# Moving ScalarE's late squares and stores, the last weight splits, and the sharing of the last scalings in a hybrid encoder block

## The chip, the cores and the metric

The kernel runs on one core of a Trainium2 chip. Its time is the device time in microseconds (us) of one execution; the median of three runs of the kernel before is 2010.85 us (2010.63 to 2011.96). A NeuronCore has a matrix engine (TensorE, PE in the profile, with its weight loads as PEld), three engines for elementwise work (VectorE or DVE, ScalarE or ACT, GpSimd or POOL) and SyncE (SP), which here only issues transfers. Sixteen DMA engines move data between the device memory and the core's own memory; transfers are issued from SP, ACT or POOL.

## The reference, cut to what matters

The input x has 512 rows of 2048 numbers in float32.

```python
h = rmsnorm(x, g_mix)
qa, ka, va, qb, kb, vb = split(h @ w_in)
mixed = concat(rmsnorm(mixer_a(qa, ka, va), g_out_a), rmsnorm(mixer_b(qb, kb, vb), g_out_b))
x = x + mixed @ w_out
h2 = rmsnorm(x, g_ffn)
gate, up = split(h2 @ w_gate_up)
x = x + (silu(gate) * up) @ w_down
return rmsnorm(x, g_final)          # x / sqrt(mean(x*x) + eps) * g_final, row by row
```

## The kernel before, in words

**Precision and form.** Every float32 product is made of three matmuls: each operand is split into a rounded part "hi" and a remainder "lo", and `mm3` (L238 to L240) adds hi·hi, hi·lo and lo·hi. So weights must be split before use: ScalarE makes hi (L774), VectorE makes lo (L777). Most of the large products also use a seven-product form for 2x2 blocks (m1 to m7), for which VectorE first adds or subtracts weight tiles (L814).

**Units.** The work of TensorE is a list of units. A unit is one weight tile (128 x 512) with the matmuls that use it: 12 matmuls in the first chunk (units 0 to 15), 6 in the seven-product blocks that follow. The last loop of the kernel runs over the units in order, and writes each engine's instructions in that order: squares of x (`row_squares`), loads and splits for units some way ahead (`prepare`), the unit's matmuls, its `post` and the hooks set for this unit number. Each engine works its own list from the top, so an instruction that must wait holds all behind it on its engine. hi runs about five units ahead in these blocks (`COLS_AHEAD`), lo one unit behind hi.

**The beginning.** The first chunk computes the k and v columns of mixer A from all 16 column slices of x. Its four result banks are copied out by ScalarE (L468, `post_plain`) and stored to device memory as kvA (L455). Beside this, slices of x are transposed and split (L333 to L335, and L352 to L357 in `x_split` and `x_sums`), and ScalarE squares x with a running sum (L369): 16 instructions, one for each column group g and row tile t. The last four (g = 3) come at units 15, 16, 17 and 18. `make_r1` at unit 20 makes 1/rms of the rows: a reduction and a scaling on VectorE, a power on GpSimd (L220), one more scaling on VectorE (L389). Its first reader is the copy of the first finished form of the next block (L862, after unit 23).

**Places.** Weight tiles, the copies of the first chunk and the tiles of x share a pool of places of 128 x 512 (`homes`). At unit 15 three are free, so the fourth copy of the first chunk goes to the place of the first one, and waits until that one is stored. The next three loads of SP's list go to the places of the second, third and fourth copy. The four places of the last group of x come free with its last square.

**The end.** The last block of the down projection ends with forms m5, m4, m3. Rows are in four tiles t of 128, columns in four chunks c of 512. After m4 the rows 2 and 3 are complete: `put_row` adds the bank to x1 (VectorE, L1200) and squares the result (ScalarE, L1197). `row_scale` makes 1/rms (reduction and scaling on VectorE, power on GpSimd), `write_rows` scales the four chunks and stores each with SP (L1222). Three chunks of each row tile have been multiplied by g_final before (`gained`, L1204), and need only the row scale; the fourth takes both at once on VectorE (L1217). Form m3 runs with rows 0 first; its second half, for rows 1, is held until the end (`finish`), so that rows 2, 3 and 0 can be finished beside it. For the last row tile, the sum over three chunks is made ahead.

Of the kernel before, what the change touches and what calls it, by code (L numbers as in the profile page):

```python
# [15 lines left out]
OP = mybir.AluOpType  # L16
# [3 lines left out]
P = 128  # L20
# [3 lines left out]
NT = S // P  # L24
KD = D // P
NC = D // 512
# [41 lines left out]
def encoder_block(ctx, tc, x, g_mix, w_in, g_q_a, g_k_a, g_out_a, g_out_b, w_out, g_ffn,  # L68
                  w_gate_up, w_down, g_final, c_ident, c_mask, c_axial, c_partial, out):
    nc = tc.nc  # L70
# [13 lines left out]
    def slot(base, dtype=F32, shape=(P, 512)):  # L84
        return sp.tile(list(shape), dtype, tag="s", name=nm(base))
# [14 lines left out]
    def release(*tiles):  # L100
        banks.extend(tiles)
# [201 lines left out]
    def hook(n, f):  # L303
        hooks.setdefault(n, []).append(f)
# [58 lines left out]
    x_ss = small(4 * NT)  # L363

    def row_squares(n):
        g, t = (3, n - KD + 1) if n >= KD - 1 else divmod(n - 3, NT)
        if 0 <= g < 4 and 0 <= t < NT:
            row = x_groups[g][:, t]
            nc.scalar.activation(row, row, AF.Square, accum_out=x_ss[:, 4 * t + g:4 * t + g + 1])  # L369
            if g in (1, 3) and t == NT - 1:  # L370
                homes.extend(x_groups[g][:, i] for i in range(NT))
# [82 lines left out]
    def store(name, t, src, eng=None):  # L454
        (eng or nc.gpsimd).dma_start(spill[name][t], src)  # L455
        stored[name] += 1
# [4 lines left out]
    def post_plain(name, ps, rows=range(NT)):  # L461
        for t in rows:
            e = homes.popleft() if name == "kvA" else slot("ev" + name)
            if name[:3] == "qkB":
                nc.scalar.activation(e[:, :256], ps[t][:, :256], AF.Copy, scale=r1["rs"][:, t:t + 1])
                nc.scalar.activation(e[:, 256:], ps[t][:, 256:], AF.Copy, scale=r1["r"][:, t:t + 1])
            else:
                nc.scalar.activation(e, ps[t], AF.Copy, scale=1.0 if name == "kvA" else r1["r"][:, t:t + 1])  # L468
# [444 lines left out]
    x1 = {}  # L913
# [194 lines left out]
    for f in range(0, NFF, 4):  # L1108
        box = gate_up_block(f)
# [31 lines left out]
    gfin = {}  # L1141
    fin = {}
    def down_block(first, pairs, cb, last):
        box = ColBlock(w_down, 2 * first * P, (cb * 1024, cb * 1024 + 512), pairs, KEPT, f"draw{pairs}",
                       close=finish if last else None)

        def add(form, i, j):
            def go():
                for t in range(2):
                    row = 2 * i + t  # L1150
                    e = in_turn(evs, EVICT, [P, 512], F32, "ev")
                    nc.scalar.activation(e, box.bank_of(form)[t], AF.Copy, scale=r2["r"][:, row:row + 1])  # L1152
                    nc.gpsimd.dma_start(x1_dram[2 * cb + j, row], e, accum_op=OP.add)  # L1153
                if form in LAST_OF_BANK:
                    box.done(form)
            box.after(form, 0, go)

        def put(form, i, j):
            box.after(form, 0, lambda: [put_row(2 + j, 2 * i + t, box.bank_of(form)[t]) for t in range(2)])

        add("m1", 0, 0)
        add("m7", 1, 1)
        add("m6", 1, 0)
        if last:
            done_rows = [(c, t) for c in range(2) for t in (2, 3, 0, 1)]
            for n in range(2):
                box.after("m7", 2 + 3 * n, lambda n=n: [load_gfin(n), load_x1(n, (2, 3)), load_x1(n, (0, 1))])
            box.after("m7", 7, lambda: [load_gfin(c) for c in (3, 2)])
            for n, (c, t) in enumerate(done_rows):
                box.after("m6", n - 2, lambda c=c, t=t: squares(c, t))  # L1170
                box.after("m6", n, lambda c=c, t=t: gained(c, t))
            box.after("m6", 2, lambda: [load_x1(3, (2, 3)), load_x1(2, (0, 1)), load_x1(2, (2, 3)), load_x1(3, (0, 1))])
            put("m2", 0, 0)
            put("m5", 1, 1)
            put("m4", 1, 0)
            for t in range(2):
                box.after("m4", -6 + t, lambda t=t: gained(2, t))
                box.after("m4", -4 + t, lambda t=t: gained(3, 2 + t))
            box.after("m4", 1, lambda: [row_scale(t) for t in (2, 3)])
        else:  # L1180
            add("m2", 0, 0)
            add("m5", 1, 1)
            add("m4", 1, 0)
            add("m3", 0, 1)
        return box

    def load_gfin(c):
        gfin[c] = slot("gfin")
        nc.gpsimd.dma_start(gfin[c], row_bcast(g_final[c * 512:(c + 1) * 512], 512))
# [9 lines left out]
    def put_row(c, t, ps):  # L1199
        nc.vector.scalar_tensor_tensor(x1[c, t], ps, r2["r"][:, t:t + 1], x1[c, t], op0=OP.mult, op1=OP.add)  # L1200
        squares(c, t)
# [7 lines left out]
        nc.vector.tensor_reduce(tot, fin[t], axis=AX.X, op=OP.add)  # L1209
        fin["r", t] = rsqrt_mean(tot, 1, D)  # L1210

    def write_rows(t, by_vector):
        r = fin["r", t]
        for c in sorted(range(NC), key=lambda c: ("y", c, t) in fin):
            y = x1[c, t]
            if ("y", c, t) not in fin:
                nc.vector.scalar_tensor_tensor(y, y, r, gfin[c], op0=OP.mult, op1=OP.mult)  # L1217
            elif c == by_vector:
# [3 lines left out]
            nc.sync.dma_start(out[0, t * P:(t + 1) * P, c * 512:(c + 1) * 512], y)  # L1222

    def finish(box):
        ps = box.bank_of("m3")
        write_rows(2, None)
        write_rows(3, None)
        put_row(3, 0, ps[0])
        for u in box.held:
            mm3(ps[1], cols(form_of("m3", u.i), P), (u.pair[:, 0], u.pair[:, 1]), False, u.i == box.pairs - 1, True)  # L1230
        row_scale(0)
        write_rows(0, None)
        pre = small(2)
        nc.vector.tensor_reduce(pre[:, :1], sums_of(1)[:, :NC - 1], axis=AX.X, op=OP.add)
        nc.vector.tensor_scalar(pre[:, 1:], pre[:, :1], 1.0 / D, EPS, op0=OP.mult, op1=OP.add)
        put_row(3, 1, ps[1])
        m = small(1)
        nc.vector.tensor_scalar(m, fin[1][:, NC - 1:NC], 1.0 / D, pre[:, 1:], op0=OP.mult, op1=OP.add)
        fin["r", 1] = small(1)
        nc.gpsimd.tensor_tensor(fin["r", 1], m, mhalf[:, :1], op=OP.pow)  # L1240
        write_rows(1, 2)

    first = 0
    for n in DOWN_PAIRS:
        next_forms(box, first, n)
        for cb in range(2):
            box = down_block(first, n, cb, (first + n, cb) == (NFF // 2, 1))
# [5 lines left out]
    done = {"load": 0, "side": 0, "hi": 0, "lo": 0}  # L1253
# [53 lines left out]
    for n, u in enumerate(units):  # L1307
        if n < KD:
            if n + 5 < KD:
                load_x(n + 5)  # L1310
            if n + 1 < KD:
                x_prep(n + 1)
            if 4 < n < 10:
                next(gains, None)
        if n < KD + 3:
            row_squares(n)
        prepare(n)
        for v in units[n + 1:n + 3]:
            if v.early is not None:
                v.early()  # L1320
                v.early = None
        u.mm(u)
        if u.post is not None:
            u.post()
        for f in hooks.pop(n, ()):
            f()
        credit = credit + HEAD_RATE[n >= attend[1]] if attend[0] <= n < attend[2] else 1.0
        while side and credit >= getattr(side[0], "cost", 1.0):
            f = side.popleft()
            credit -= getattr(f, "cost", 1.0)  # L1330
            f()
        if not side:
            credit = 0.0
# [54 lines left out]
```

## Time and profile before

| | |
|---|---|
| median of three runs | 2010.85 us (2010.63 to 2011.96) |
| the profiled execution | 2011.22 us, of which the span is 2009.4 us and 1.8 us lie around it |
| granted TensorE clock | 0.997 |
| PE busy | 1984.8 us, 99% |
| VectorE, ScalarE, GpSimd busy | 1562.4, 1114.6 and 127.4 us |
| moved by DMA | 390.61 MB, mean 194 GB/s |

The profile shows one execution. Times in its rows are us from the span's start. A row of the timeline gives start, duration, engine, source line, operation, and output and input by the program's names; in brackets stands the idle time of the engine before it, and whose end released it. Rows of the same kind that follow each other are merged, with their count (x2); the duration is then that of the whole stretch. The letter q behind an engine means its instruction queue (waits and DMA issues). Matmuls are pipelined: the duration of one overlaps the next, so the distance of two starts is what counts.

### The profile page before, as it was taken

The page shows a single profiled execution, that of the slowest core. Times are in us where ns is not written, and L with a number is a line of the kernel's source. Part 1 is how long each engine was busy: PE and PEld are TensorE (multiplying, and loading weights), DVE is VectorE, ACT ScalarE, POOL GpSimd, SP SyncE. Part 2 cuts the span into 40 slices and gives each one's busy share as a digit, 9 for nine tenths or more (in the row PEclk, how much of TensorE's full clock was granted, in tenths as well). Part 3 has the DMA queues.
Part 4 walks back from the last instruction along what each step waited for, and adds up shares of the span by engine and source line. Part 5 has one row for each costly group of instructions (what it writes and reads, how often), then busy time and mean ns, then how long its engine had stood idle before and what let it go on. Part 6 is the DMA issues. An engine that isn't in the chain of part 4 may idle for free. (4 is left out here: it accounts for less than half of the span.)

```text
span 2009.4 us, 27417 instructions
## 1 busy us (share of the span) xinstructions
PE 1984.8 (99%) x9019; PEld 1632.0 (81%) x9019; DVE 1562.4 (78%) x2781; ACT 1114.6 (55%) x1988; POOL 127.4 (6%) x157
## 2 busy tenths in 40 slices
PE   9999999999999999999999999999999999999998
PEld 7788888887788888888888888888888888788886
DVE  6877876667764698878878878878779987877967
ACT  8655345456544565555555545455555666666656
POOL 0000100000010000000000000000000121111121
PEclk9999999999999999999999999999999999999999
DMA  8577433335344645737647657558467799768765
GB/s 274 179 276 249 159 116 99 106 129 169 96 140 132 209 153 188 279 119 258 241 135 273 208 178 275 168 189 287 141 221 262 195 248 272 187 169 266 200 152 175
DMA packets 231391, 390.61 MB, mean 194 GB/s; under 512 B 21408, under 2 KB 70352, under 8 KB 231120
## 3 DMA queue, kind: packets, MB, share of 16 engines
q1 hardware_dynamic: 204880, 326.13, 48.4%
q0 software_dynamic: 14960, 33.04, 8.1%
q10 hardware_dynamic: 11408, 29.70, 4.2%
q8 instruction: 70, 1.15, 0.2%
q14 instruction: 73, 0.60, 0.1%
HBM read 325.08 MB, written 63.70 MB: 193 GB/s over the span
## 5 line engine op out<-in xcount | busy, mean ns | idle before, releaser
L238 PE MATMUL b<-tw,arena 128*128 128x512 f32 x2136 | 838.4, 392 | 2.2 <-ACT ev L1152 2.2
L239 PE MATMUL b<-tw,arena 128*128 128x512 f32 x2136 | 833.6, 390 | 2.8 <-DVE tw L777 2.6
L240 PE MATMUL b<-tw,arena 128*128 128x512 f32 x2136 | 832.9, 390 | 0.0
L774 ACT ACTIVATE tw<-raw 128x512 fp32r<-128x512 f32 x924 | 558.6, 628 | 436.6 <-DVE raw L814 285.9
L777 DVE TENSOR_TENSOR tw<-raw,tw 128x512 fp32r<-128x512 f32 x924 | 617.8, 685 | 172.4 <-ACT tw L774 169.5
L239 PEld LDWEIGHTS b<-tw,arena 128*128 128x128 f32 x2136 | 401.7, 188 | 89.2 <-DVE tw L777 7.4
L238 PEld LDWEIGHTS b<-tw,arena 128*128 128x128 f32 x2136 | 401.5, 188 | 84.6 <-ACT ev L1152 2.9
L240 PEld LDWEIGHTS b<-tw,arena 128*128 128x128 f32 x2136 | 401.4, 188 | 84.5 <-DVE arena L330 0.5
L814 DVE TENSOR_TENSOR raw<-raw,raw 128x512 f32<-128x512 f32 x528 | 360.5, 683 | 2.0 <-DMA raw<-in_w_gate_up_dram 2.0
L238 PE MATMUL b<-w,arena 128*128 128x512 f32 x368 | 146.1, 397 | 0.0
L239 PE MATMUL b<-w,arena 128*128 128x512 f32 x368 | 143.6, 390 | 0.7 <-DVE w L295 0.7
L240 PE MATMUL b<-w,arena 128*128 128x512 f32 x368 | 143.8, 391 | 0.0
L1153 POOL DMA_DIRECT2D x1d<-ev x76 | 66.4, 975 | 1150.0 <-ACT ev L1152 1135.6
L239 PEld LDWEIGHTS b<-w,arena 128*128 128x128 f32 x368 | 69.2, 188 | 15.3 <-DVE w L295 1.6
L240 PEld LDWEIGHTS b<-w,arena 128*128 128x128 f32 x368 | 69.1, 188 | 14.9
L238 PEld LDWEIGHTS b<-w,arena 128*128 128x128 f32 x368 | 69.2, 188 | 13.5
L774 ACT ACTIVATE tw<-stage 128x512 fp32r<-128x512 f32 x93 | 55.6, 627 | 41.0 <-DVE stage L814 30.6
L777 DVE TENSOR_TENSOR tw<-stage,tw 128x512 fp32r<-128x512 f32 x93 | 61.5, 684 | 13.6 <-ACT tw L774 13.6
L295 DVE TENSOR_TENSOR w<-raw,w 128x512 fp32r<-128x512 f32 x96 | 64.7, 684 | 6.0 <-ACT w L290 3.5
L230 DVE TENSOR_TENSOR pTl<-b,pTh 128x512 fp32r<-128x512 f32 x64 | 43.8, 686 | 29.6 <-ACT pTh L229 26.9
L290 ACT ACTIVATE w<-raw 128x512 fp32r<-128x512 f32 x96 | 58.3, 623 | 15.5 <-PE b L239 6.9
L357 DVE TENSOR_TENSOR pair<-pair 128x256 f32<-128x256 f32 x120 | 45.5, 420 | 26.2 <-ACT pair L1009 25.1
(189 smaller groups left out, 1748.9 us busy)
## 6 DMA issues: line engine op xcount, KB each, us to landing
raw<-in_w_gate_up_dram SPq DMA_DIRECT2D x616, 256.0 KB, 5.3
raw<-in_w_down_dram SPq DMA_DIRECT2D x176, 256.0 KB, 7.1
stage<-in_w_in_dram SPq DMA_DIRECT2D x114, 256.0 KB, 4.8
forms<-pair SPq DMA_DIRECT2D x22, 896.0 KB, 5.3
x1d<-ev POOLq DMA_DIRECT2D x76, 256.0 KB, 6.7
fr<-forms ACTq DMA_DIRECT2D x35, 512.0 KB, 6.1
raw<-in_w_in_dram SPq DMA_DIRECT2D x64, 256.0 KB, 4.4
raw<-in_w_out_dram SPq DMA_DIRECT2D x32, 512.0 KB, 4.7
```

Of the source, the lines that this page charges most:

```text
L230: nc.vector.tensor_tensor(lo, src, f32(hi), op=OP.subtract)
L238: nc.tensor.matmul(dst, ah, bh, start=start, stop=False, skip_group_check=chained)
L239: nc.tensor.matmul(dst, ah, bl, start=False, stop=False, skip_group_check=chained)
L240: nc.tensor.matmul(dst, al, bh, start=False, stop=stop, skip_group_check=chained)
L290: nc.scalar.activation(self.w[0], src, AF.Copy)
L295: nc.vector.tensor_tensor(self.w[1], self.src, f32(self.w[0]), op=OP.subtract)
L357: nc.vector.tensor_tensor(out, x, y, op=op)
L774: nc.scalar.activation(self.pair[:, 0], self.src, AF.Copy)
L777: nc.vector.tensor_tensor(self.pair[:, 1], self.src, f32(self.pair[:, 0]), op=OP.subtract)
L814: nc.vector.tensor_tensor(t[dst], t[src[0]], t[src[1]], op=OP.add if form == "m6" else OP.subtract)
L1153: nc.gpsimd.dma_start(x1_dram[2 * cb + j, row], e, accum_op=OP.add)
```

## The change

1. `row_squares`: the last four squares of x come at units 17, 19, 21 and 23 instead of 15 to 18, and `make_r1` at unit 23 instead of 20.
2. `post_plain`: the four stores of the first chunk are issued by GpSimd instead of ScalarE.
3. `last_weights`: after the last unit of form m4, and ahead of everything else that is hooked there, the hi and lo splits of all weights that are left are written.
4. `write`, `finish`: the scalings and stores of the end are written chunk by chunk. For rows 2 and 3 the chunk that takes both factors comes first, then two on ScalarE, and the last on VectorE behind `put_row(3, 0)`. For rows 0, one of three single scalings goes to VectorE. For rows 1 the fourth chunk is multiplied by g_final (into the place of another gain tile) while ScalarE squares it; VectorE then scales three chunks, ScalarE one, which ScalarE also stores.

```diff
     def row_squares(n):
-        g, t = (3, n - KD + 1) if n >= KD - 1 else divmod(n - 3, NT)
+        g, t = divmod(n - 3, NT)
+        if g >= 3:
+            late = n - KD - 1
+            g, t = (3, late // 2) if late >= 0 and late % 2 == 0 else (-1, 0)
...
-    hook(20, make_r1)
+    hook(23, make_r1)
...
-            store(name, t, e, nc.scalar)
+            store(name, t, e, None if name == "kvA" else nc.scalar)
...
             put("m5", 1, 1)
+            box.after("m4", 0, last_weights)
             put("m4", 1, 0)
...
+    def last_weights():
+        while done["hi"] < len(units):
+            units[done["hi"]].split_hi()
+            done["hi"] += 1
+        while done["lo"] < len(units):
+            units[done["lo"]].split_lo()
+            done["lo"] += 1
...
-    def write_rows(t, by_vector):
...
+    def write(t, c, vector, queue):
+        r, y = fin["r", t], x1[c, t]
+        if ("y", c, t) not in fin:
+            nc.vector.scalar_tensor_tensor(y, y, r, gfin[c], op0=OP.mult, op1=OP.mult)
+        else:
+            y = y if fin["y", c, t] is True else fin["y", c, t]
+            if vector:
                 nc.vector.tensor_scalar(y, y, r, None, op0=OP.mult)
             else:
                 nc.scalar.activation(y, y, AF.Copy, scale=r)
+        queue.dma_start(out[0, t * P:(t + 1) * P, c * 512:(c + 1) * 512], y)
 
     def finish(box):
         ps = box.bank_of("m3")
-        write_rows(2, None)
-        write_rows(3, None)
+        for t in (2, 3):
+            write(t, 2, True, nc.sync)
+            for c in (0, 1):
+                write(t, c, False, nc.sync)
         put_row(3, 0, ps[0])
+        for t in (2, 3):
+            write(t, 3, True, nc.sync)
...
         row_scale(0)
-        write_rows(0, None)
+        write(0, 3, True, nc.sync)
+        for c in (0, 1):
+            write(0, c, False, nc.sync)
+        write(0, 2, True, nc.sync)
...
         put_row(3, 1, ps[1])
+        nc.vector.tensor_tensor(gfin[0], x1[3, 1], gfin[3], op=OP.mult)
+        fin["y", 3, 1] = gfin[0]
...
-        write_rows(1, 2)
+        write(1, 0, True, nc.sync)
+        write(1, 2, False, nc.scalar)
+        write(1, 1, True, nc.sync)
+        write(1, 3, True, nc.sync)
...
-        if n < KD + 3:
+        if n < KD + 8:
             row_squares(n)
```

ScalarE's list before, from the split of unit 19 to the splits of units 22 and 23 (L468 copies out the first chunk's banks, L455 stores them, L369 squares x, L774 makes hi, L352 splits forms of x):

```order
L774 ACTIVATE tw_161<-stage 128x512
L468 ACTIVATE stage<-b_75 128x512
L455 DMA kvA<-stage 128x512
L468 ACTIVATE stage<-b_76 128x512
L455 DMA kvA<-stage 128x512
...
L369 ACTIVATE stage,smalls<-stage 128x512
L774 ACTIVATE tw_161<-stage 128x512 x2
L352 ACTIVATE arena_85<-xpair_168 128x256
L352 ACTIVATE arena_86<-xpair_168 128x256
L352 ACTIVATE arena_86<-xpair_168 128x2x256
L369 ACTIVATE stage,smalls<-stage 128x512
L774 ACTIVATE tw_161<-stage 128x512
```

The same place of the changed kernel, where L471, L372 and L777 are what L468, L369 and L774 were:

```order
L777 ACTIVATE tw_161<-stage 128x512
L471 ACTIVATE stage<-b_75 128x512
L471 ACTIVATE stage<-b_76 128x512
L471 ACTIVATE stage<-b_77 128x512
L471 ACTIVATE stage<-b_78 128x512
L777 ACTIVATE tw_161<-stage 128x512 x2
L352 ACTIVATE arena_85<-xpair_168 128x256
L352 ACTIVATE arena_86<-xpair_168 128x256
L352 ACTIVATE arena_86<-xpair_168 128x2x256
L372 ACTIVATE stage,smalls<-stage 128x512
L777 ACTIVATE tw_161<-stage 128x512 x2
```

The four stores have left this list, and the square between the copies and the splits of units 20 and 21 stands behind the splits of x. The stores stand in GpSimd's list, between its last store of x's forms and the power of `make_r1`.

VectorE's list before, from the last rows' sums of rows 2 and 3 (L1200) to their first full scalings (L1217); the names tw are split weights, raw their sources:

```order
L777 TENSOR_TENSOR tw_6038<-raw_15990,tw_6038 128x512
L1200 SCALAR_TENSOR_TENSOR x_1539_16314<-b_71,smalls,x_1539_16314 128x512
L1200 SCALAR_TENSOR_TENSOR x_1540_16316<-b_75,smalls,x_1540_16316 128x512
L777 TENSOR_TENSOR tw_6039<-raw_16006,tw_6039 128x512
L1209 TENSOR_REDUCE smalls<-smalls 128x1
...
L777 TENSOR_TENSOR tw_6040<-raw_16018,tw_6040 128x512
L1217 SCALAR_TENSOR_TENSOR x_1539_16314<-x_1539_16314,smalls,gfin_16256 128x512
```

The same place of the changed kernel (L780 is what L777 was, L1212, L1221 and L1227 what L1200, L1209 and L1217 were):

```order
L780 TENSOR_TENSOR tw_6038<-raw_15990,tw_6038 128x512
L780 TENSOR_TENSOR tw_6039<-raw_16006,tw_6039 128x512
L780 TENSOR_TENSOR tw_6040<-raw_16018,tw_6040 128x512
L1212 SCALAR_TENSOR_TENSOR x_1539_16314<-b_71,smalls,x_1539_16314 128x512
L1212 SCALAR_TENSOR_TENSOR x_1540_16316<-b_75,smalls,x_1540_16316 128x512
L1221 TENSOR_REDUCE smalls<-smalls 128x1
```

The two last lo splits stand ahead of the rows' sums instead of behind them.

More of the change, by code (lines that the diff above doesn't have):

```diff
@@ L1210, in row_scale @@
         fin["r", t] = rsqrt_mean(tot, 1, D)
-    def write_rows(t, by_vector):
[L1213 to L1218, printed above, removed]
+    def write(t, c, vector, queue):
[5 more added lines that the diff above has]
+            if vector:
                 nc.vector.tensor_scalar(y, y, r, None, op0=OP.mult)
@@ L1221, in write_rows @@
                 nc.scalar.activation(y, y, AF.Copy, scale=r)
-            nc.sync.dma_start(out[0, t * P:(t + 1) * P, c * 512:(c + 1) * 512], y)
+        queue.dma_start(out[0, t * P:(t + 1) * P, c * 512:(c + 1) * 512], y)
     def finish(box):
         ps = box.bank_of("m3")
-        write_rows(2, None)
-        write_rows(3, None)
+        for t in (2, 3):
+            write(t, 2, True, nc.sync)
+            for c in (0, 1):
+                write(t, c, False, nc.sync)
         put_row(3, 0, ps[0])
+        for t in (2, 3):
+            write(t, 3, True, nc.sync)
         for u in box.held:
```

## The prediction

> **What bounds the kernel now.** I read the page first, then who waits on PE, then the two places that the change touches.
>
> ```profile
> PE 1984.8 (99%) x9019; PEld 1632.0 (81%) x9019; DVE 1562.4 (78%) x2781; ACT 1114.6 (55%) x1988; POOL 127.4 (6%) x157
> ```
>
> PE is the bound: it is busy 99% of the span. A change of other engines can win only where PE waits, and behind PE's last matmul. The edits touch one stretch of waits, after the first chunk (PE's timeline):
>
> ```profile
> 63.07 0.40 PE L238 MATMUL b<-tw,arena 128*128 128x512 f32 x1
> 63.64 0.50 PE L239 MATMUL b<-tw,arena 128*128 128x512 f32 x1 [0.17 <-DVE tw L777]
> ...
> 64.67 0.39 PE L240 MATMUL b<-tw,arena 128*128 128x512 f32 x1
> 64.90 0.40 PE L238 MATMUL b<-tw,arena 128*128 128x512 f32 x1
> 65.90 0.50 PE L239 MATMUL b<-tw,arena 128*128 128x512 f32 x1 [0.60 <-DVE tw L777]
> ...
> 67.18 0.39 PE L238 MATMUL b<-tw,arena 128*128 128x512 f32 x1
> 67.96 0.50 PE L239 MATMUL b<-tw,arena 128*128 128x512 f32 x1 [0.39 <-DVE tw L777]
> ...
> 69.23 0.40 PE L238 MATMUL b<-tw,arena 128*128 128x512 f32 x1
> 69.84 0.50 PE L239 MATMUL b<-tw,arena 128*128 128x512 f32 x1 [0.21 <-DVE tw L777]
> ...
> 71.10 0.39 PE L238 MATMUL b<-tw,arena 128*128 128x512 f32 x1
> ```
>
> Undisturbed starts are 0.227 apart (64.67, 64.90), six to a unit: 1.36. Units 20 to 23 start at 63.07, 64.90, 67.18 and 69.23, unit 24 at 71.10: 8.03 instead of 5.44, **2.6 us** lost. Each time it is the unit's second matmul that waits, the first that needs lo; from it to the next unit are 1.27 (63.64 to 64.90, 69.84 to 71.10). VectorE makes those lo late:
>
> ```profile
> 62.89 0.69 DVE L777 TENSOR_TENSOR tw<-stage,tw 128x512 fp32r<-128x512 f32 x1 [3.03 <-ACT tw L774]
> 63.72 1.52 DVE L353 TENSOR_TENSOR arena<-xpair,arena 128x256 fp32r<-128x256 f32 x3
> 65.16 0.68 DVE L777 TENSOR_TENSOR tw<-stage,tw 128x512 fp32r<-128x512 f32 x1
> ...
> 67.22 0.68 DVE L777 TENSOR_TENSOR tw<-stage,tw 128x512 fp32r<-128x512 f32 x1
> ...
> 69.10 1.28 DVE L777 TENSOR_TENSOR tw<-stage,tw 128x512 fp32r<-128x512 f32 x2
> ```
>
> VectorE idles 3.03 us until unit 20's hi, and then is full: lo of units 20, 21, 22, 23 start at 62.89, 65.16, 67.22, 69.10. So ScalarE sets the start of the row of waits, VectorE its length. ScalarE was here:
>
> ```profile
> 57.51 0.58 ACT L468 ACTIVATE stage<-b 128x512 f32<-128x512 f32 x1
> ...
> 60.59 0.60 ACT L468 ACTIVATE stage<-b 128x512 f32<-128x512 f32 x1 [0.46 <-PE b L240]
> 61.21 0.36 ACTq L455 DMA_DIRECT2D kvA<-stage  x1
> 61.62 0.63 ACT L369 ACTIVATE stage<-stage 128x512 f32<-128x512 f32 x1 [0.43 <-ACT stage L468]
> ...
> 62.25 1.14 ACT L774 ACTIVATE tw<-stage 128x512 fp32r<-128x512 f32 x2
> ```
>
> **The change, first place.** Unit 15's square (0.6) goes from ahead of the copies, so the first copy starts at about 56.9 and ends at 57.5 instead of 58.1. The fourth copy goes to the first one's place and must wait for that store, now GpSimd's. Before no GpSimd store of a ScalarE copy stands in this stretch; the nearest row is one six us earlier, with DMA idle too:
>
> ```profile
> 50.81 0.69 DVE L335 TENSOR_TENSOR arena<-xpair,arena 128x512 fp32r<-128x512 f32 x1 [0.55 <-ACT arena L334]
> 51.92 0.54 POOL L338 DMA_DIRECT2D ar<-arena  x1 [5.99 <-DVE arena L335]
> ar<-arena POOLq DMA_DIRECT2D x1, 256.0 KB, 2.3
> vB<-ends POOLq DMA_DIRECT2D x4, 256.0 KB, 5.8
> 56.00:58.00 2.00, 2.00 (x10) 1.65 (x9) 1.93 (x5) 2.00 (x5) 0.00 (x0) 1.00 0.00 0
> ```
>
> GpSimd issues 0.4 after its producer's end (51.50 to 51.92), and that transfer lands 2.3 after the issue; stores of this size among heavy loads have a median of 5.8. I take 2.3, since DMA stands idle at this point too (the last row is the stretch 56 to 58, and its last two columns are DMA's share and GB/s), and keep 5.8 as the other end. Issue at 57.9, landing at 60.2, so the fourth copy starts at 60.25 (60.59 before), and the splits of units 20 and 21 follow 0.58 later, at 60.83. Before, an issue of 0.4 and a square of 0.63 stood between, until 62.25. Gain on ScalarE: **1.4 us**.
>
> Now forward. lo 20 runs 61.5 to 62.2, before PE wants it (63.07 + 0.23): no wait. The L353 row starts when ScalarE's first L352 ends (two hi of 0.52 and 0.4 behind 60.83), at 62.3, and lo 21 follows at 63.74 (distance 1.44 as in the rows), ends 64.4; PE wants it at 64.66: no wait. lo 22 comes 2.06 behind lo 21 as before (65.16 to 67.22), at 65.80, and is usable at 66.54 (0.74 from lo's start to PE's, as 67.22 to 67.96); PE wants it at 66.02: wait 0.52, and unit 23 starts at 66.54 + 1.27 = 67.81. lo 23 comes 1.88 behind lo 22 (67.22 to 69.10), at 67.68, usable 68.42; PE wants it at 68.04: wait 0.4. Unit 24 starts at 68.42 + 1.27 = 69.7 instead of 71.1, and lo 24 is there. Gain: **1.4 us**. It could be 2.6 if VectorE gets through its list faster than I count, and less if ScalarE starts later (the rivals).
>
> The squares reappear behind the splits of x, 0.6 each; they and the splits of units 22 to 28 fill ScalarE until 70.4. The three lo splits that now stand ahead of r1's reduction put it at 70.7 (70.30 before, three times 0.6 more, and lo 23 starts 1.4 sooner), and r1 where it was plus 0.4:
>
> ```profile
> 70.76 1.04 POOL L220 TENSOR_TENSOR smalls<-smalls,fixed 128x4 f32<-128x4 f32 x1 [18.30 <-DVE smalls L218]
> 71.83 1.27 ACT L862 ACTIVATE ends<-b,smalls 128x512 f32<-128x512 f32 x2 [1.26 <-POOL smalls L220]
> ```
>
> Behind the waiting L862 stand the hi splits from unit 29. They start at 73.4, and lo 29 is done at 74.7; PE wants it at 69.7 + 5 x 1.36 + 0.23 = 76.7. The cover of this wait is 2.0 us, so I cost it at nothing. Loads: the squares' four places come free later, so units 32 and 33 are loaded into places that come free with lo 24 (about 69.0) and at once behind it, some 3 us later than before.
>
> ```profile
> stage<-in_w_in_dram SPq DMA_DIRECT2D x114, 256.0 KB, 4.8
> ```
>
> They land from 73.8 on, and VectorE's subtraction for unit 32 comes at 75.2; PE reaches that unit at 69.7 + 8 x 1.36 = 80.6. I cost this too at nothing; without that cover each us would cost one. GpSimd idled for 18.30 us ahead of 70.76, so its four issues delay only who waits for the stores: the fourth copy, and SP's next three loads, which waited for ScalarE's stores before.
>
> **Second place, the end.**
>
> ```profile
> 1992.48 0.39 PE L238 MATMUL b<-tw,arena 128*128 128x512 f32 x1
> ...
> 1994.28 0.50 PE L239 MATMUL b<-tw,arena 128*128 128x512 f32 x1 [0.22 <-DVE tw L777]
> ...
> 1994.84 0.39 PE L238 MATMUL b<-tw,arena 128*128 128x512 f32 x1
> 1990.82 1.40 DVE L1200 SCALAR_TENSOR_TENSOR x<-b,smalls,x 128x512 f32<-128x512 f32 x2
> 1992.14 0.68 DVE L777 TENSOR_TENSOR tw<-raw,tw 128x512 fp32r<-128x512 f32 x1
> ...
> 1993.53 0.69 DVE L777 TENSOR_TENSOR tw<-raw,tw 128x512 fp32r<-128x512 f32 x1 [0.17 <-ACT tw L774]
> 1994.91 0.34 SPq L1222 DMA_DIRECT2D out_dram<-x  x1
> 2000.50 0.75 DVE L1200 SCALAR_TENSOR_TENSOR x<-b,smalls,x 128x512 f32<-128x512 f32 x1 [0.30 <-PE b L240]
> 2005.08 0.40 SPq L1222 DMA_DIRECT2D out_dram<-x  x1
> ```
>
> From 1992.48 to 1994.84 PE does two units of three matmuls, 1.36 of work in 2.36: it loses 1.0 around the last two splits; with both ahead of the sums it loses none (the last hi split moves into idle time of ScalarE ahead of its squares). But that 1.0 doesn't reach the end. In the old time scale: the sums start two splits (1.2) later, 1992.02; 0.4 comes back where the reduction had stood behind the first split, 0.4 where the scaling had stood behind the second. First store: 1994.91 + 1.2 - 0.8 = 1995.35. From there the stores are a row for DMA:
>
> ```profile
> 1996.00:2003.50 7.50, 5.43 (x11) 1.00 1.05 378
> 2003.50:2004.50 1.00, 0.74 (x2) 1.00 0.60 225
> ```
>
> (Stretch, length, ScalarE busy, granted clock, DMA share, GB/s.) DMA is full at 378 GB/s until 2003.5, and the next stretch of 1.0 us has 225, a hole of 1 - 225/378 = 0.4 us before the last row tile. 16 stores of 256 KB are 4.19 MB, 11.1 us at 378. The new scalings close the hole: last issue 1.0 earlier (2004.05), long before DMA gets to it. So the end moves by +0.44 (first store) and -0.4 to -0.5 (hole): **-0.1**, and not by PE's 1.0, which is the other end. VectorE too gives back only 0.3: the last sum at 2000.50 waited for PE, and now waits for a scaling that VectorE took over. The Trainium skill, page "DMA: Bandwidth & Descriptors", section "Specifications", gives about 358 GB/s as one core's limit of the device memory; by that figure the row would take an estimated 11.7 us and the sum would be 0.6 less gain. The row above shows 378, and it decides.
> **Sum:** 1.4 + 0.1 = 1.5 off the profiled 2011.22 (span 2009.4 and 1.8 around it), so 2009.7; the median of the runs stands 0.37 under the profiled execution, so 2010.85 - 1.5 = **2009.35**. A measurement here tells about 0.2%, 4 us, from no change.
>
> **Rivals.**
> *The tail pays in full.* If DMA isn't the limit at the end, the last issue's 1.0 counts: 1.4 + 1.0, 2008.45. Against it: a share of 1.05 over 7.5 us. With the stall gone wholly (2.6) too: 2007.25, the best case.
> *GpSimd's store holds ScalarE* (slower). The fourth copy waits for its landing, and everything behind waits too. If it lands 3.7 after the issue (61.6), the splits of units 20 and 21 start at 62.25 as before, and from there each us costs one. At 5.8 they start at 64.3, 2.1 late: 2010.85 + 2.1 - 0.1 = 2012.9. For it: that median. Against it: DMA is idle here.
> The Trainium skill has a mechanism for it: "SBUF — State Buffer", section "SBUF: two separate sides", says that GpSimd can't write its transfers' descriptors while VectorE runs an operation in a two-port mode, and shows 620 ns becoming 3100. By that figure the landing would come an estimated 2.5 later, at 4.8, and the time would be 2011.9. The row of 2.3 was taken beside VectorE's two-input operations, as here, so I give it 0.03 of this rival's chance.
> *r1 becomes late.* It needs over 2.0 us beyond my count; each us beyond costs one; with 2 beyond it is 2009.35 + 2 = 2011.35.
> *The change doesn't do what it says.* VectorE alone sets the four waits, and they merely start later: 2010.85 - 0.1 = 2010.75.
>
> **Numbers.** Forecast 0.50 (2008.7 to 2010), full tail 0.17, GpSimd's store 0.15, nothing won 0.11, late r1 0.05, something else 0.02. The range takes in the full tail with over half of the stall's other 1.2, and the store's rival but for its last 0.6: 2007.6 to 2012.3. All but the rarest cases stay within 4 us: faster by over 0.2% 0.04, slower 0.05, within 0.91.
>
> **What would show it.** Right: PE's waits at units 20 and 21 gone, about 0.5 each left at 22 and 23, unit 24 at 69.7; the fourth copy at 60.2; PE's last wait gone; out stores without a hole, and the last landing hardly moved against PE's end plus 1. Wrong: a fourth copy after 61.7, a wait of PE at unit 29, or a hole among the stores.

## The result and the profile after

| | before | changed |
|---|---|---|
| median, both on one chip, 20 runs each | 2012.46 us (2010.63 to 2016.39) | 2008.95 us (2007.22 to 2013.71) |
| ratio | | 0.9985, 95% interval 0.9979 to 0.9991 |
| the profiled execution, its span | 2011.22 us, 2009.4 | 2008.06 us, 2006.3 |
| VectorE, ScalarE busy | 1562.4, 1114.6 us | 1565.2, 1113.2 us |

By the ratio the gain is 3.0 us (1.8 to 4.2); the two medians lie 3.5 apart. That is inside the 4 us under which a measurement of this kernel is not told from no change by itself; with 20 runs on each side it shows. The forecast was a gain of 1.5. That its time, 2009.35, stands close to 2008.95 is in good part luck, for two errors cancel: the median of 20 runs of the kernel before is 1.6 us above the 2010.85 from which the sum started, and between the medians stands a gain of 2.0 us that the prediction did not have.

**First place.** PE's rows of the changed kernel, units 20 to 24 (in this execution PE runs 0.19 us later than in the old one when it gets here; take that off to compare):

```profile
63.25 0.39 PE L238 MATMUL b<-tw,arena 128*128 128x512 f32 x1
...
64.61 0.40 PE L238 MATMUL b<-tw,arena 128*128 128x512 f32 x1
...
66.00 0.40 PE L238 MATMUL b<-tw,arena 128*128 128x512 f32 x1
66.70 0.50 PE L239 MATMUL b<-tw,arena 128*128 128x512 f32 x1 [0.31 <-DVE tw L780]
...
67.96 0.40 PE L238 MATMUL b<-tw,arena 128*128 128x512 f32 x1
68.58 0.50 PE L239 MATMUL b<-tw,arena 128*128 128x512 f32 x1 [0.22 <-DVE tw L780]
...
69.86 0.39 PE L238 MATMUL b<-tw,arena 128*128 128x512 f32 x1
```

Units 20 and 21 take 1.36 and 1.39, undisturbed. Units 22 and 23 wait once each: their second matmuls start 0.70 and 0.62 behind the first instead of 0.23, so 0.47 and 0.39 late. Unit 24 starts at 69.86, in the old scale 69.67, where it was 71.10. ScalarE and GpSimd behind it:

```profile
57.09 1.54 ACT L471 ACTIVATE stage<-b 128x512 f32<-128x512 f32 x3
60.48 0.60 ACT L471 ACTIVATE stage<-b 128x512 f32<-128x512 f32 x1 [1.86 <-DMA kvA<-stage]
60.98 1.14 ACT L777 ACTIVATE tw<-stage 128x512 fp32r<-128x512 f32 x2
58.06 1.74 POOL L458 DMA_DIRECT2D kvA<-stage  x3 [5.42 <-ACT stage L471]
71.30 1.04 POOL L220 TENSOR_TENSOR smalls<-smalls,fixed 128x4 f32<-128x4 f32 x1 [9.28 <-DVE smalls L218]
72.38 1.26 ACT L865 ACTIVATE ends<-b,smalls 128x512 f32<-128x512 f32 x2 [1.22 <-POOL smalls L220]
```

and the DMA issues between 50 and 75 (count, size, median us to landing):

```profile
kvA<-stage POOLq DMA_DIRECT2D x4, 256.0 KB, 2.7
```

Three copies run without issues between them. ScalarE then idles 1.86 us for the store, which is issued at 58.06 and is down by 60.48: 2.4 us. The fourth copy follows, and the splits behind it.

**The end.** VectorE, SP and PE of the changed kernel:

```profile
1996.90 0.75 DVE L1212 SCALAR_TENSOR_TENSOR x<-b,smalls,x 128x512 f32<-128x512 f32 x1
1992.16 8.58 SPq L1234 DMA_DIRECT2D out_dram<-x  x14
2000.84 1.13 SPq L1234 DMA_DIRECT2D out_dram<-gfin  x1
1995.84 0.39 PE L240 MATMUL b<-tw,arena 128*128 128x512 f32 x1
```

and two stretches of it (columns as before, the last two DMA's share and GB/s):

```profile
1993.25:2000.75 7.50, 2.97 (x14) 2.12 (x12) 5.54 (x15) 4.07 (x9) 1.08 (x2) 0.85 1.06 366
2000.75:2001.75 1.00, 0.00 (x0) 0.00 (x0) 0.00 (x0) 0.00 (x0) 0.00 (x0) 0.50 1.05 402
```

PE's last wait is gone, and no hole is left among the stores: the stretch that stood at 225 GB/s stands at 402. The last transfer lands at 2005.36 (2008.28 before), 13.20 us after the first store's issue (13.37 before).

**A third place.** Neither the prediction nor the change speaks of the down projection at 1680 to 1722, but PE's waits on VectorE there are gone. The view of waits for PE, 1675 to 1724, before (who waits for whom, us in total, times, longest):

```profile
PE b L239 <- DVE tw L777: 1.0, 3, 0.6
```

The same view of the changed kernel has no row. With the stalls around each wait counted, as at the first place, it is 2.1 us.

Where the time came from is read best matmul by matmul: both traces hold 9019 of them in the same order, so the start of each in the one less that in the other shows where lead is won. By places of the old execution:

| stretch of the old execution | lead won (-) or lost (+), us | what stands there |
|---|---|---|
| to 62 | +0.19 | start |
| 62 to 80 | -1.50 | units 20 to 24 |
| 80 to 470 | +0.18 | |
| 470 to 510 | +1.19 | clock at half for 6.83 us, before for 3.41 |
| 510 to 1680 | -0.01 | |
| 1680 to 1722 | -2.14 | waits of the down projection |
| 1722 to 1735 | -1.71 | before, clock at half for 3.41 us; now not |
| 1735 to 1985 | +0.58 | single waits |
| 1985 to the last landing | +0.30 | the end |
| sum | -2.92 | last landing 2008.28 to 2005.36 |

The two rows on the clock differ from execution to execution of one kernel (last section), and so do the single waits: a second execution of the changed kernel has -0.01 at 80 to 470 and +0.09 at 1735 to 1985. What stays in both executions is 1.5 and 2.1 won, and 0.3 or more lost at the end.

### The profile page after: what moved, and what is told of

It is laid out like the page before. It is cut to its first block, busy times and chain, and to the rows that moved or that the text cites. A ratio compares the mean times of both kernels' runs of the same rounds, so it can differ in the third digit from the quotient of the medians.

```text
span 2006.3 us, 27422 instructions
## 1 busy us (share of the span) xinstructions
PE 1982.6 (99%) x9019; PEld 1632.3 (81%) x9019; DVE 1565.2 (78%) x2786; ACT 1113.2 (55%) x1984; POOL 129.1 (6%) x161
## 4 chain that ended last, share of the span: by engine, by line
PE 92%; DVE 3%; issue 2%; ACT 2%; DMA 1%; POOL 0%; ACTq 0%; POOLq 0%; DVEq 0%
PE b L238 29%; PE b L239 29%; PE b L240 29%; PE b L583 1%; DVE tw L780 1%; PE b L1084 1%; DVE raw L817 1%; DMA x<-x1d 0%; PE b L1009 0%; PE b L319 0%; PE b L545 0%; DVE pTl L230 0%; DMA oA<-oT 0%; POOL x1d L1156 0%; DMA oB<-oT 0%
## 5 line engine op out<-in xcount | busy, mean ns | idle before, releaser
L777 ACT ACTIVATE tw<-raw 128x512 fp32r<-128x512 f32 x924 | 559.1, 628 | 433.3 <-DVE raw L817 282.7
L780 DVE TENSOR_TENSOR tw<-raw,tw 128x512 fp32r<-128x512 f32 x924 | 618.7, 686 | 169.8 <-ACT tw L777 166.6
L777 ACT ACTIVATE tw<-stage 128x512 fp32r<-128x512 f32 x96 | 58.0, 628 | 40.2 <-DVE stage L817 29.4
L238 PEld LDWEIGHTS b<-w,arena 128*128 128x128 f32 x368 | 69.1, 188 | 13.5
L780 DVE TENSOR_TENSOR tw<-stage,tw 128x512 fp32r<-128x512 f32 x96 | 64.0, 686 | 12.2 <-ACT tw L777 12.1
```

What stands on the lines that cost most here:

```text
L238: nc.tensor.matmul(dst, ah, bh, start=start, stop=False, skip_group_check=chained)
L777: nc.scalar.activation(self.pair[:, 0], self.src, AF.Copy)
L780: nc.vector.tensor_tensor(self.pair[:, 1], self.src, f32(self.pair[:, 0]), op=OP.subtract)
```

## The experiments

The theory from the first two profiles: the beginning's edits have the gain, and the stores hide what the end's edits give PE. The rivals: the end has a share of it, or VectorE and not DMA holds the end. What won 2 us in the down projection was open. Each kernel was run beside the kernel before on one chip. The table gives the ratio of the times, and from each profiled execution the lead at the same stretches, against the profiled execution of the kernel before. The kernel before and the changed kernel were each profiled a second time (again).

| kernel | ratio of times (95%) | 62 to 80 | 470 to 510 | 1680 to 1722 | 1722 to 1735 | end |
|---|---|---|---|---|---|---|
| before, again | | 0.00 | -1.02 | +0.32 | -1.59 | +0.09 |
| changed | 0.9985 (0.9979 to 0.9991) | -1.50 | +1.19 | -2.14 | -1.71 | +0.30 |
| changed, again | | -1.52 | -0.19 | -2.13 | -1.82 | +0.81 |
| e_begin | 0.9986 (0.9977 to 0.9995) | -1.53 | -1.00 | -1.90 | 0.00 | +0.47 |
| e_end | 1.0001 (0.9992 to 1.0009) | 0.00 | +0.01 | +0.44 | -1.66 | +0.22 |
| e_weights | 1.0000 (0.9991 to 1.0009) | -0.01 | +0.04 | +0.50 | -1.65 | -0.30 |
| e_share | 0.9994 (0.9985 to 1.0003) | 0.00 | 0.00 | +0.06 | -1.59 | +0.26 |
| e_fourth | 0.9976 (0.9966 to 0.9987) | -2.70 | -0.99 | -1.78 | -1.59 | +1.05 |
| e_fewer | 0.9988 (0.9979 to 0.9997) | -1.53 | +1.06 | -2.09 | -0.01 | +0.03 |
| e_squares | 0.9980 (0.9971 to 0.9989) | -1.30 | -1.03 | -2.13 | -1.68 | +0.38 |
| e_stores | 1.0002 (0.9993 to 1.0010) | -0.21 | +0.06 | +0.30 | -1.58 | -0.44 |
| e_place | 0.9992 (0.9983 to 1.0001) | +0.01 | +0.03 | -1.88 | -1.62 | +0.79 |
| e_back | 0.9985 (0.9976 to 0.9994) | -1.54 | -1.68 | +1.90 | -1.57 | +0.33 |

**Beginning or end.** e_begin has edits 1 and 2 alone, e_end edits 3 and 4.

```diff
 # e_begin: before, with
+    hook(23, make_r1), the late squares of row_squares, and
+            store(name, t, e, None if name == "kvA" else nc.scalar)
 # e_end: the changed kernel, with these three as before
```

> The kernel before with the two edits of the beginning alone (later squares and r1, first chunk's stores on GpSimd). Theory (the gain is made at the beginning, the end gives about nothing): unit 24 starts 1.3 to 1.5 us sooner than before, and the time falls by 1.4 or by what the whole change brought (3.0, interval 1.8 to 4.2), whichever cause adds the rest. Rival (the beginning and the end bring half each): the time falls by 1.4 and the rest is missing. In the profile both want PE's waits at units 20 and 21 gone and about 0.5 left at each of 22 and 23.

> The kernel before with the two edits of the end alone (last weights ahead, last scalings shared anew). Theory (stores fill DMA at the end): PE ends 1.0 us sooner against the start of form m3, but the last landing stands 0 to 0.4 us later against the same point, so the time is within 0.5 of before. Rival (the end brings the half that the forecast lacked): 1.5 less, to 2.0 less.

e_begin came out at 2009.23 us beside 2011.53, e_end at 2012.17. The beginning's two edits have the whole gain (0.9986, the changed kernel 0.9985), the end's two none that shows.

**ScalarE's wait for the store.** In e_fourth the fourth copy gets a place of its own.

```diff
-            e = homes.popleft() if name == "kvA" else slot("ev" + name)
+            e = homes.popleft() if name == "kvA" and t < NT - 1 else slot("ev" + name)
...
-            if name == "kvA":
+            if name == "kvA" and t < NT - 1:
                 homes.append(e)
```

> The changed kernel with a place of its own for the fourth copy of the first chunk, so that ScalarE waits for no store there. Theory (ScalarE's wait for the store sets the rest of PE's waits): hi of units 20 and 21 start 1.8 us sooner, all lo up to unit 23 are in time, PE's two waits of 0.5 go, unit 24 starts 1.2 us sooner than in the changed kernel, and the time is 1.2 less. Rival (VectorE's own list sets the waits at units 22 and 23): the two waits stay and the time is the same as the changed kernel's. Units 29 to 31 have then at most 1 us of cover left for r1, so a wait at unit 29 of up to 0.5 is possible in both.

It came out at 2007.27 us beside 2011.53, the lowest median of this study. ScalarE's rows of e_fourth (this execution is 0.71 later than the old one at this place, the changed kernel's 0.19):

```profile
57.62 1.55 ACT L471 ACTIVATE stage<-b 128x512 f32<-128x512 f32 x3
59.05 0.60 ACT L471 ACTIVATE evkvA<-b 128x512 f32<-128x512 f32 x1
59.53 1.16 ACT L777 ACTIVATE tw<-stage 128x512 fp32r<-128x512 f32 x2
```

The splits of units 20 and 21 follow at 59.53 (58.82 in the old scale, before 62.25), PE waits nowhere between 56 and 80, and 2.70 us are won. So the 1.2 that the change leaves at the first place are ScalarE's wait for the store; VectorE alone would keep pace if it started in time.

**The stores at the end.** e_fewer is the changed kernel without the stores of row tile 2: rows 256 to 383 of the output are not written, 12 stores instead of 16.

```diff
-        queue.dma_start(out[0, t * P:(t + 1) * P, c * 512:(c + 1) * 512], y)
+        if t != 2:
+            queue.dma_start(out[0, t * P:(t + 1) * P, c * 512:(c + 1) * 512], y)
```

> The changed kernel without the stores of row tile 2, so rows 256 to 383 of the output aren't written: 12 stores of 256 KB instead of 16. Theory (the row of stores through DMA sets the end): the last landing comes 2.0 to 2.6 us sooner against PE's last matmul (4 x 0.67 less, until the last store's own issue and 2.4 us to landing decide), and the time is 2.0 to 2.6 less than the changed kernel's. Rival (the chain of sums, powers and scalings sets it): no difference.

2009.06 us: no gain, as the rival said. The profile shows why. VectorE and SP of e_fewer (PE's last matmul starts at 2000.79):

```profile
2002.49 0.75 DVE L1212 SCALAR_TENSOR_TENSOR x<-b,smalls,x 128x512 f32<-128x512 f32 x1
1998.74 7.49 SPq L1235 DMA_DIRECT2D out_dram<-x  x10
2006.32 0.46 SPq L1235 DMA_DIRECT2D out_dram<-gfin  x1
```

and the stretch of its stores:

```profile
1999.80:2006.30 6.50, 1.37 (x7) 0.79 (x5) 4.91 (x13) 3.12 (x7) 1.08 (x2) 1.00 0.90 314
```

DMA is no longer full (314 GB/s), and the last landing comes 11.30 us after the first store instead of 13.2. But the first store itself is that of row tile 3 now, later in the program, and the last sum stands 1.70 us behind PE's last matmul (2002.49 against 2000.79; 1.06 in the changed kernel, 0.42 before): VectorE reaches it late. From PE's last matmul to the last landing it is 9.25, in the changed kernel 9.53. So two things seem to hold the end, the stores and VectorE's list, and taking one away wins 0.3. The second is read from these rows; no run takes work off VectorE there. In all thirteen executions with 16 stores, two of them of the kernel before, the last landing stands 13.2 to 13.5 us behind the first store's issue.

**The end's two edits apart.** e_weights has the last weights alone (edit 3), e_share the new sharing alone (edit 4); with them both kernels were profiled once more.

```diff
 # e_weights: before, with
+            box.after("m4", 0, last_weights)
 # e_share: before, with write() and finish() of the changed kernel
```

> The kernel before with the last weights' splits ahead of the finished rows, and nothing else. Theory: PE's 1.0 us of waits at the last two units of m3 go, the first store comes 0.4 to 0.6 later against the start of m3, DMA still has its hole before the last row tile or a smaller one; the time is within 0.5 of before. Rival (PE's end carries through): 1.0 less.

> The kernel before with the new order and sharing of the last scalings and stores, and nothing else. Theory: PE's 1.0 us of waits at m3's last units stay, the hole of 0.4 us among the stores closes, and the time is 0.4 to 0.6 less than before, at most. Rival (stores aren't the limit, the last scaling chain is): 0.8 to 1.0 less.

> The kernel before once more, unchanged, for a second profile. Theory (executions of one kernel differ by when late weight loads land in the down projection and by how many half-clock stretches of 3.4 us PE gets): the waits at units 20 to 23 are the same as in the first profile, within 0.1, while the waits of ScalarE for a load at about 1687 (4.9 us in the first profile) and the half-clock stretches (two, at 482 and 1728) may differ. Rival (these belong to the kernel's order): 4.9 us, two stretches and the same places again.

> The changed kernel once more, unchanged, for a second profile. Theory: unit 24's start and the tail within 0.2 of the first profile, while the wait for a load at about 1684 (2.6 us) and the half-clock stretches (6.8 us at 480, none at 1726) may differ. Rival (these belong to the changed order): 2.6 us and the same stretches again.

Measured 2011.43 and 2011.61 us beside 2011.9: neither tells itself from no change. In e_weights PE's last wait is gone and PE ends 1.02 us sooner, and 0.3 of it arrive; in e_share PE's last wait stays, and the last landing comes 0.1 closer to the first store (13.27 against 13.37). Both are too small to be told from the scatter of the column "end". The second executions gave 2009.31 for the kernel before and 2006.6 for the changed one: 2.7 between them, but each 2 us or more under its median, so a single execution proves little here. The first place repeats within 0.02; of the kernel before the second execution has neither of the two half-clock stretches behind PE's waits near 482 and 1728, as the theory allowed.

**What won 2 us in the down projection.** Down to e_fewer, the table shows -1.8 to -2.1 at 1680 to 1722 in each kernel with edits 1 and 2, and no gain without. Both edits stand 1600 us earlier. SP's list says what changed: its waits between 1625 and 1660 in the kernel before, and in the changed one.

```profile
SPq L267 <- DVE tw L777: 20.1, 2, 19.9
```

```profile
SPq L267 <- DMA fr<-forms: 15.8, 4, 6.9
SPq L267 <- DMA raw<-in_w_down_dram: 10.5, 8, 5.6
SPq L267 <- DVE tw L780: 4.3, 3, 2.9
```

Before, SP stands still for 19.9 us, from 1634 to 1653.9, with one load (the program's raw_1388) that waits for VectorE's last use of its place; everything behind it on SP waits too. In the changed kernel this and the five loads behind it go out from 1634 on:

```profile
1634.00 10.07 SPq L267 DMA_DIRECT2D raw<-in_w_down_dram  x6
```

DMA in the two stretches 1633.9 to 1653.8 and 1655 to 1685, before and then changed:

```profile
1633.90:1653.80 19.90, 19.90 (x89) 16.52 (x88) 18.88 (x31) 13.00 (x21) 3.50 (x4) 1.00 0.79 176
1655.00:1685.00 30.00, 30.00 (x134) 24.86 (x133) 22.78 (x34) 18.75 (x31) 6.97 (x8) 1.00 1.03 316
```

```profile
1633.90:1653.80 19.90, 19.90 (x89) 16.47 (x89) 18.89 (x30) 12.95 (x21) 3.50 (x4) 1.00 0.94 249
1655.00:1685.00 30.00, 30.00 (x134) 24.83 (x133) 22.75 (x34) 19.59 (x33) 6.96 (x8) 1.00 0.99 288
```

Before, DMA has a share of 0.79 while SP stands, and is full (1.03) right after; the loads are late, ScalarE idles 4.94 us for one, VectorE for ScalarE, and VectorE's list is behind when PE wants its splits from 1698 on. ScalarE of before and of the changed kernel:

```profile
1686.79 1.16 ACT L774 ACTIVATE tw<-raw 128x512 fp32r<-128x512 f32 x2 [4.94 <-DMA raw<-in_w_down_dram]
```

```profile
1684.42 1.15 ACT L777 ACTIVATE tw<-raw 128x512 fp32r<-128x512 f32 x2 [2.60 <-DMA raw<-in_w_down_dram]
```

The built programs show the same in SP's list, before and then changed (DVE: the load waits for VectorE as well as for a transfer):

```
raw_1388<-in_w_down_dram 128x512 [waits DMAHW1,DVE]
raw_1394<-in_w_down_dram 128x512 [waits DMAHW7]

raw_1388<-in_w_down_dram 128x512 [waits DMAHW5]
raw_1394<-in_w_down_dram 128x512 [waits DMAHW3,DVE]
```

raw_1388 takes the place of raw_1367 before, and that of raw_1366, long free, in the changed kernel; raw_1367's place goes to raw_1394, six loads later. The order of instructions is the same there; only the places that the memory planner gives out have moved, because tiles at the beginning live longer or start later. That the places decide the wait is theory A of four runs; rival B is that they don't, and the stores' way or something else does it.

```diff
 # e_squares: before, with edit 1 alone
+            late = n - KD - 1
+            g, t = (3, late // 2) if late >= 0 and late % 2 == 0 else (-1, 0)
 # e_stores: before, with edit 2 alone
+            store(name, t, e, None if name == "kvA" else nc.scalar)
 # e_place: before, with
-    hook(21, lambda: more_homes("more", ...
+    hook(22, lambda: more_homes("more", ...
 # e_back: the changed kernel, with
-    hook(21, lambda: more_homes("more", ...
+    hook(20, lambda: more_homes("more", ...
```

> Edit 1 alone: the late squares, with the four stores still on ScalarE, and the end as before. Theory A: the part of the gain that the prediction missed (PE gains 1.8 to 2.1 us between 1680 and 1722 in each profile with edits 1 and 2, none without) comes with edit 1, because it changes which places the pool gives to later loads: load 1388 of the down projection no longer takes a place whose last reader is VectorE at about 1654. It expects -2.0 there again, and at the first place: copies from 56.9, the fourth about 2.5 us after the first store's issue (58.12 to 60.59 before), so at 60.0, its store's issue of 0.4 behind it, the splits of units 20 and 21 at 61.0 instead of 62.25, gain 1.2. Sum -3.2 us against the kernel before, without half-clock stretches. Rival B: the missed part comes with the stores' way (edit 2). It expects -1.2 in all, and PE's waits at 1698 to 1722 as before.

> Edit 2 alone: the four stores on GpSimd, the squares where they were. Theory A: no change of the places, so PE's waits at 1698 to 1722 stay as before; at the first place the copies run from 57.5 without issues between them, the store is issued at 58.5 and lands at 60.8, the fourth copy starts at about 60.85, the square of 0.63 follows it, the splits of units 20 and 21 come at 62.05 instead of 62.25: gain 0.2. Sum -0.2 us, not to be told from no change. Rival B: -0.2 at the first place and -2.0 between 1680 and 1722: -2.2 us.

> The kernel before with one number changed: the four extra places (more) are handed out after unit 22 instead of 21. No square, store, split or scaling moves; the built program then gives every weight load of the down projection that was looked at the same place as the changed kernel does. Theory A: nothing changes at units 20 to 24 (PE's four waits as before, 2.6 us lost there), the six loads 1388 to 1393 are issued from 1634 on instead of 1654, PE's waits at 1698 to 1722 go: -2.0 us against the kernel before. Rival B (the places don't matter, the stores or the earlier PE do): no change, 0.

> The changed kernel with one number changed: the four extra places are handed out after unit 20 instead of 21. Load 1388 of the down projection then waits for the same late reader on VectorE as in the kernel before; all four edits stay. Theory A: the first place keeps its gain of 1.5, the loads from 1388 on are issued at about 1654 again and PE's waits at 1698 to 1722 come back: 2.0 us slower than the changed kernel, -1.0 to -1.5 against the kernel before, which is what the prediction had counted. Rival B: as the changed kernel, -3.0.

e_squares won 4.0 us by the ratio (2.2 to 5.8; its median is 2008.16 beside 2011.34), 1.30 at the first place and 2.13 in the down projection. e_stores won nothing (2011.43): 0.21 and a loss of 0.30. ScalarE's rows of e_squares (1.6 later than the old execution here) and of e_stores (1.24 later) show the two halves:

```profile
61.60 0.60 ACT L471 ACTIVATE stage<-b 128x512 f32<-128x512 f32 x1 [0.46 <-DMA kvA<-stage]
62.63 1.15 ACT L777 ACTIVATE tw<-stage 128x512 fp32r<-128x512 f32 x2 [0.43 <-ACT stage L471]
```

```profile
62.16 0.60 ACT L468 ACTIVATE stage<-b 128x512 f32<-128x512 f32 x1 [1.86 <-DMA kvA<-stage]
63.27 1.14 ACT L774 ACTIVATE tw<-stage 128x512 fp32r<-128x512 f32 x2
```

In the old scale the splits come at 61.03 and 62.03, as expected (61.0 and 62.05). e_place moved nothing but the places, kept PE's four waits at units 20 to 23, and won its 1.88 between 1680 and 1722; its time is 1.6 us lower, with an interval from 3.4 lower to 0.2 higher. SP's longest wait for VectorE fell as in the changed kernel, and in e_back it came back. SP's row of e_place, then SP's and PE's rows of e_back:

```profile
SPq L267 <- DVE tw L777: 5.9, 4, 3.3
```

```profile
SPq L267 <- DVE tw L780: 21.6, 2, 20.2
PE b L239 <- DVE tw L780: 1.7, 4, 0.6
PE b L238 <- ACT tw L777: 0.7, 1, 0.7
```

So the places decide PE's waits there in both directions: shown. But e_back is no mere return. At 1680 to 1722 it stands 1.90 behind the kernel before, where theory A asked for none: PE waits 2.4 us there instead of 1.0, and in its built program the five loads ahead of raw_1388 wait for VectorE too, which none of them does in the kernel before. And its time does not follow: theory A asked for -1.0 to -1.5, and 2008.85 us is as fast as the changed kernel (-3.0, interval -4.8 to -1.2). Its profile says why in part: the earlier hand-out moves other places as well, and PE's waits of 0.7 and 0.5 around 455 and 478 are gone, 1.0 and 0.6 us of lead; nor has it the half clock behind 480. That the 2 us of the down projection show in the time as well rests on e_squares against e_stores and, within its interval, on e_place; e_back does not bear it out, and how much of its time is its own gain at 455 to 480, and how much chance, stays open.

## Why the prediction was right, and where it was wrong

**First place: right, step by step.** In the old scale the fourth copy starts at 60.29 (forecast 60.25), its store's issue to landing is 2.4 (2.3), the splits follow at 60.79 (60.83), the waits at units 20 and 21 are gone, those at 22 and 23 are 0.47 and 0.39 (0.52 and 0.4), unit 24 starts at 69.67 (69.7), and 1.5 are won (1.4). r1 came 0.35 later (forecast 0.4), and PE did not wait at unit 29. The rival in which GpSimd's store holds ScalarE beyond 61.6 fell: 60.29. By the Trainium skill, page "SBUF — State Buffer", section "SBUF: two separate sides", the landing would have come an estimated 2.5 us later if VectorE had run an operation in a two-port mode; the landing took 2.4 us in all. Beside it stood VectorE's two-input operations alone, and whether one of them runs in such a mode no run here shows, so the page's case stays untested. What the text did not say is how unequal the two edits are: the squares alone win 1.3, the stores alone 0.2.

**Second place: right in kind, off by 0.4.** First store in the old scale 1995.38 (forecast 1995.35). PE's last wait is gone, PE ends 1.02 sooner, the end does not move with it, and the hole is closed. But closing it gave back 0.17 and not 0.4 to 0.5: the row of stores ran at 366 GB/s over the 7.5 us in which it had stood at 378. So the end lost 0.3 where 0.1 was to be won; kernels with the old end scatter from -0.44 to +0.79 there, so no more than "nothing" is shown. The prediction's own terms gave nothing too: +0.44 and -0.4 to -0.5 make +0.04 to -0.06 and not -0.1, and 1994.91 + 1.2 - 0.8 is 1995.31 and not 1995.35. The reason was also half of it: e_fewer's rows show VectorE's list as a second cover of about the same length. The 358 GB/s of the Trainium skill ("DMA: Bandwidth & Descriptors", "Specifications") is no limit here: 366 over 7.5 us and 402 over the next 1.0. The 0.6 that the prediction would have taken off the gain by that figure would stand in both kernels, and cancel.

**The step that failed** is the one on the loads: "the squares' four places come free later, so units 32 and 33 are loaded into places that come free with lo 24 ... I cost this too at nothing". For units 32 and 33 that held: PE waits nowhere from 72 to 82. But a place that changes hands moves the whole row of places behind it, and the text followed two loads and not the row. In its place the runs show one load of the down projection that no longer waits 19.9 us for its place, worth 1.8 to 2.1 us of PE's waits. The sum should have been 1.5 + 2.1 - 0.3 = 3.3; measured 3.0 (1.8 to 4.2). From the profile of before the price was there to see: a transfer queue that stands 19.9 us on one wait with DMA at 0.79, and is full behind it. That the change would touch it could be seen only in SP's list and its waits, not in the code.

The likeliest case stood at 2008.7 to 2010 and the result is 2008.95. Counted as gains it is further off: the case spans 0.85 to 2.15, the measured gain is 3.0, and the full tail (2.4, or 2008.45) lies nearer. The tail's mechanism fell: in the changed kernel and in e_end PE ends 1.02 sooner, and the last landing is 0.30 and 0.22 later.

## What to carry to other kernels

Where a planner gives out memory, a small edit moves the places of all that comes later: before costing an edit at nothing, compare the waits of the transfer queue in both programs to the end, and look in the profile for the longest wait of that queue behind which DMA runs full. One such wait, 1600 us away from the edit, was worth more lead here than the edit's own purpose (1.9 alone in e_place, against 1.5). A stall that is started by one engine and lengthened by another went wholly when the first got a free start (e_fourth: 2.7 us, where 2.6 had been counted as lost); taking work off the first engine's list alone won half of it (e_squares: 1.3). And a gain of PE just ahead of the row of stores was worth nothing that shows: in all thirteen executions with 16 stores the end stands 13.2 to 13.5 us behind the first store.

## What the runs showed of the hardware

Identical work ran at half clock for 0, 3.41 or 6.83 us behind the same wait of PE. PE's row and then the stretch behind it (the granted clock is the number before DMA's share), first of the kernel before, then of the changed kernel:

```profile
481.56 0.65 PE L580 MATMUL b<-fixed,p 128*128 128x128 f32 x4 [2.42 <-DVE pTl L230]
```

```profile
482.30:486.40 4.10, 4.10 (x13) 3.20 (x12) 3.06 (x7) 2.43 (x6) 0.00 (x0) 0.58 0.15 16
```

```profile
480.43 1.11 PE L583 MATMUL b<-fixed,p 128*128 128x128 f32 x4 [2.43 <-DVE pTl L230]
```

```profile
482.30:486.40 4.10, 4.10 (x11) 3.20 (x10) 3.19 (x8) 2.43 (x7) 0.00 (x0) 0.50 0.20 57
```

Of the fourteen profiled executions seven have one stretch of 3.41 us behind this wait, two have 6.83, five none. Behind a wait of 1.7 us near 1726 three of fourteen have one, and e_fewer has one more behind a wait of 1.9 us near 541. By the table of stretches one costs 1.0 us at the first of these waits and 1.6 to 1.8 at the second. That is a good part of the 5.8 us between the fastest and the slowest of the 20 runs of the kernel before. The Trainium skill, page "TensorE: Matmul & The Clock Gate", section "What's actually happening", gives a free-running window of 3413 ns: the length agrees. That a window's phase decides which executions get a stretch would fit the counts, but no run here shows it. Its advice in "Why this matters for your kernels", no idle gaps over about 3 us, is not enough here: the stretches stand behind waits of 1.7 to 2.4 us.
